# Keeping Newton iterates and row norms in PSUM in a hand-scheduled hybrid decoder layer, with the order planned again

## Chip, cores and metric

The kernel runs on one core of a Trainium2 chip. The time is device microseconds of one execution, median of several runs. Five engines run their own instruction queues side by side: PE (TensorE: matrix products into the accumulator memory PSUM), DVE (VectorE), ACT (ScalarE), POOL (GpSimd) and SP (SyncE, here the issuer of DMAs). [...]

## Reference

One decoder layer is applied to a prompt of 1024 tokens and to 8 sample tokens with caches. All data are float32. Cut to what the change touches:

```python
def rmsnorm(x, g):
    return x * lax.rsqrt(jnp.mean(x * x, axis=-1, keepdims=True) + NORM_EPS) * g

def decoder_layer(...):
    h = x + 0.5 * rmsnorm(swiglu(rmsnorm(x, n_ffn1_pre), ffn1_gate, ffn1_up, ffn1_down), n_ffn1_post)
    u = rmsnorm(h, n_mix_pre)
    proj = u @ w_in                    # q, k, v of group A, one row of 1792 for group B
    ...                                # partial rotary embedding
    ya = attend(q, k_all, v_all, ...)  # p = softmax(map 0) - lam * softmax(map 1), 4 heads
    ya = rmsnorm(ya, subln) * (1.0 - lam_init)
    yb, s_new, shift_new = rwkv7_time_mix(pb, prev, s0, lp)
    mix = concat([ya, yb]) @ w_out
    h = h + rmsnorm(mix, n_mix_post)
    h = h + 0.5 * rmsnorm(swiglu(rmsnorm(h, n_ffn2_pre), ffn2_gate, ffn2_up, ffn2_down), n_ffn2_post)

def rwkv7_time_mix(pb, prev, s0, lp):
    ...
    kk = kk / jnp.maximum(jnp.sqrt(jnp.sum(kk * kk, -1)), 1e-12)    # per head of 64
    s, y = wkv_scan(s0, r, decay, k, v, kk, a)                      # matrix state, 8 heads
    mean = jnp.mean(y, -1); var = jnp.mean(jnp.square(y - mean), -1)
    y = (y - mean) * lax.rsqrt(var + GN_EPS) * ln_x_w + ln_x_b      # per head
    ...
```

D_MODEL is 1024, the feed-forward width 2816, the two groups are 512 wide each, the past of a sample token 512.

## Kernel before

**Stages.** Tokens lie along the free axis in chunks of 256 or 264 columns, two chunks to a half of the prompt. There are four feed-forward phases: 0 and 1 are the first network for the two halves, 2 and 3 the second. `s_trunk` (L934) runs gate, up and down products of all phases (tiles `trunk_m`, `trunk_aux` in PSUM, sums of the outputs in `trunk_xl`, sums of squares in `trunk_acc`). A product is three matmuls of high and low parts, so each weight tile of 1024 columns is split on ACT (high part) and on DVE or POOL (low part: `wts_w`, `lin_w`). Behind each phase `s_tail` (L1165) takes one chunk at a time: norm of the output (`rstd`, L704: a matmul with `init_onesD`, a square root on ACT, a reciprocal on DVE), then `post` (L743: eight scalar_tensor_tensor on DVE and eight additions), then the next norm's input as high and low parts `tail_T` or `tail_xl`, which `s_project` (L1340, `proj_m`) multiplies. For group B, eight jobs of 128 tokens (`s_job`, L1556; `job`, L1565) make the delta-rule state; `init_ind` matmuls sum the squares of the keys, a Newton iteration on DVE (`rsqrt`, L712, on tiles of 128x8) turns them into a norm (`job_stf`), and near the end of a job the group norm needs the same again (`job_st`). `attend` (L2179) makes softmax rows, `s_finish` (L2233) the heads' norm (a Newton iteration on 128x4), `s_out`, `s_outnorm` (L1371, L1425) the output projection and its norm. The sample tokens' attention (`dec_cb`, `dec_dreg`; `a_decode`, L2260) and state step (`decb_dec`, `decb_dreg`; `b_decode`, L1901) run in between.

**Order.** These generators are streams. The kernel is built in dry passes; in each, a list scheduler (`run`, L456) takes the streams' instructions by due times (`latest`, L533), with a price for each (`price`, L362) and a table `BIAS` that shifts a stream's due time by so many microseconds. `price` knows that an operation of DVE with two wide SBUF inputs keeps POOL off and the other way round (`o.port`), and `either` (L406) puts a subtraction or addition on DVE or POOL by that account. PASSES is 3, and the plan with the smallest planned end is built. The result is one fixed order for every engine. All instructions are recorded at line 301 of before (305 of the changed file), so the views tell them apart by tiles.

A PSUM tile has one of eight banks of 512 columns; a stream owns names of banks (`m0`... , `aux0`, `aux1`, `cb`, `dec`), and a new tile in a bank waits for the last reader of the one before.

Of the kernel before, what the change touches and what calls it, by code (L numbers as in the profile page):

```python
# [22 lines left out]
P = 128  # L23
# [13 lines left out]
FOUR = 1  # L37
PARTS = 2
# [7 lines left out]
C = 64  # L46
# [45 lines left out]
PASSES = 3  # L92
BIAS = {"trunk2": 300, "outn3": -70, "outb0": 30, "pre2": 7, "prep1": 60, "resid0": -60, "outn1": -10, "pre3": 30, "outn0": 3, "pre1": 3, "job13": 60, "ldxb0": -60}
# [59 lines left out]
HOP = {"tensor": (0.0, 0.2, 0.2, 0.22, 0.2), "vector": (0.18, 0.127, 0.13, 0.155, 0.13), "scalar": (0.165, 0.14, 0.143, 0.165, 0.15),  # L153
# [42 lines left out]
class Kern:  # L196
# [159 lines left out]
    @staticmethod  # L356
    def after(d, o):

        return d.seen + HOP[d.eng][ENGINES.index(o.eng)] - (o.load if d.eng == "tensor" else 0.0) + MARG * (d.eng != o.eng)

    @staticmethod
    def price(o, op, a, k, out, ins):  # L362
# [30 lines left out]
        elif o.eng == "vector":  # L393
            wide = [x for x in ins if tuple(x.shape[1:]) != (1,) and x.space != PSUM]
            fast = op in ("tensor_copy", "tensor_scalar", "memset") and all(x.space != PSUM for x in (out, *ins)) and len(wide) < 2

            o.port = fast or len(wide) > 1
            o.cost = 0.07 + n / (160 if op == "reciprocal" else 480 if op == "tensor_tensor_scan" else 1920 if fast else 960) \
                + (0.05 if op == "scalar_tensor_tensor" else 0.06 * scalars)
        elif o.eng == "scalar":  # L400
            o.cost = (0.06 if ins[0].space == PSUM else 0.093) + n / 1195 + 0.093 * scalars + 0.093 * ("accum_out" in k)
        else:
            o.port = True
            o.cost = (0.2 if op == "scalar_tensor_tensor" else 0.156 if op == "tensor_tensor" else 0.06) + n / (470 if op == "tensor_tensor" else 960)

    def either(self, op, out, *a, engines=("vector", "gpsimd")):  # L406

        if self.cur is not None:
            best = None
            for e in engines:  # L410
                o = Op(e, None, None)
                self.price(o, op, (out,) + a, {}, out, [x for x in a if isinstance(x, bass.AP)])
                t = max(self.free[e], self.held["gpsimd" if e == "vector" else "vector"] if o.port else 0.0) + self.backlog[e] + o.cost
                if e == "gpsimd" and o.port:

                    t += o.cost
                if best is None or t < best[0]:
                    best = t, e
            engines = best[1:]
        eng = getattr(self.nc, engines[0])  # L420
        getattr(eng, "copy" if op == "tensor_copy" and engines[0] == "scalar" else op)(out, *a)
# [34 lines left out]
    def run(self):  # L456
# [5 lines left out]
        while self.streams:  # L462
# [52 lines left out]
            if o.dma:  # L515
                rings = max(rings, s + (1.69 if o.eng == "gpsimd" else 1.17)) + o.dma
                o.seen = rings + 2.0
# [40 lines left out]

    def split(self, raw, tag, a, parts=1):
# [3 lines left out]
        for i in range(0, n, n // parts):  # L563
            t = slice(i, i + n // parts)
            self.nc.scalar.copy(h[:, t], raw[:, t])
            self.either("tensor_tensor", l[:, t], raw[:, t], h[:, t].bitcast(F32), ALU.subtract)
# [137 lines left out]
    def rstd(self, acc, eps=0, scale=1.0):  # L704

        nc = self.nc
        ps = self.ps2()[:, :acc.shape[-1]]
        nc.tensor.matmul(ps, self.onesD, acc, start=True, stop=True)
        nc.scalar.activation(acc, ps, AF.Sqrt, bias=self.eps[:, eps:eps + 1], scale=scale)
        nc.vector.reciprocal(acc, acc)  # L710
# [223 lines left out]
    def s_trunk(self):  # L934
# [3 lines left out]
        for ph in range(4):  # L938
# [181 lines left out]
            if ph == 3:  # L1120
                self.cur.banks = few + ("aux1",)
# [43 lines left out]
    def s_tail(self, ph, c, acc, y):  # L1165
# [26 lines left out]
        self.post(acc, y, f"n_ffn{1 + ph // 2}_post", h0 + o, z, rs)  # L1192
# [372 lines left out]
    def job(self, pool, i, s, jb):  # L1565
# [613 lines left out]
    def attend(self, pool, rd, ii, b):  # L2179
# [10 lines left out]
        for j in range(2):  # L2190
# [12 lines left out]
            V.tensor_scalar(mx[:, j, 0:1], mx[:, j, 0:1], -0.125, None, ALU.mult)  # L2203
# [29 lines left out]
    def s_finish(self, pool, half):  # L2233
# [3 lines left out]
        for rd in range(4 * half, 4 * half + 4):  # L2237
# [275 lines left out]
```

## Time and profile before

| | |
|---|---|
| median of 3 runs | 2349.36 us (2342.42 to 2352.55) |
| the profiled execution, its own time | 2346.93 us |
| its span in the trace | 2345.1 us |
| mean granted TensorE clock | 0.983 |
| POOL busy | 1069.0 us (46%) |
| HBM read, written | 254.86 MB, 41.46 MB |

Outside the span lie 1.83 us of the profiled execution. "Busy" of an engine is its share of the span; tenths in the page's second part show in which fortieth of it the engine works. A row of the trace's timeline gives start, length, engine, line, operation, out<-in by tiles, shapes and count, and in brackets the idle time ahead with what ended it. The kernel has stages with different limits, so stretches of 10 and 100 us are read apart.

### The profile page before, as it was taken

To read this page: it belongs to the slowest core of one execution; us is meant where nothing else is said; L and a number is where in the kernel's file an instruction comes from. 1 tells how busy PE (TensorE), PEld (TensorE's weight loads), DVE (VectorE), ACT (ScalarE), POOL (GpSimd) and SP (SyncE) were. 2 spreads that over 40 slices of the span, in tenths; PEclk is the share of its full clock that TensorE was granted. 3 is DMA by queue.
4 is the path that set the end of the run, shared out by engine and by line. 5 is a ranking of instruction groups with operands and counts; after the bars stand their busy time and mean duration, and the time that the engine had idled before them with its cause. 6 is when DMAs were issued, how large, how long until landed. Compare 5 with 4: busy or idle time off the path is not lost.

```text
span 2345.1 us, 42680 instructions
## 1 busy us (share of the span) xinstructions
PE 2247.0 (96%) x15871; PEld 1996.0 (85%) x15871; DVE 1658.5 (71%) x3616; ACT 1078.9 (46%) x2182; POOL 1069.0 (46%) x868
## 2 busy tenths in 40 slices
PE   7999999999999999999899998999999999999998
PEld 6999999898887778898778866777777988999998
DVE  6587898846776776838874278765777577777786
ACT  5643444543444345434452235553566556444444
POOL 5454564543333665346641133433434365444444
PEclk9999999999999999999899999999999999999999
DMA  6423333444333674635544376323535534423332
GB/s 201 129 82 100 100 106 112 125 145 127 102 102 111 190 231 137 188 109 180 168 131 144 113 168 154 86 69 96 151 105 137 175 108 132 134 64 109 109 100 73
DMA packets 454520, 299.12 MB, mean 128 GB/s; under 512 B 81033, under 2 KB 414957, under 8 KB 454312
## 3 DMA queue, kind: packets, MB, share of 16 engines
q1 hardware_dynamic: 453704, 294.78, 43.9%
q8 instruction: 126, 2.06, 0.4%
q0 software_dynamic: 320, 1.08, 0.1%
q14 instruction: 82, 0.67, 0.1%
q10 hardware_dynamic: 288, 0.52, 0.1%
HBM read 254.86 MB, written 41.46 MB: 126 GB/s over the span
## 4 chain that ended last, share of the span: by engine, by line
PE 58%; DVE 8%; ACT 3%; DMA 2%; issue 2%; POOL 1%; SPq 1%; DVEq 0%; POOLq 0%; ACTq 0%
PE trunk_m L301 32%; PE proj_m L301 7%; PE trunk_aux L301 5%; PE job_aux L301 4%; PE out_m L301 2%; PE outb_m L301 2%; PE attn_m L301 2%; PE attn_aux L301 2%; DVE mix_T L301 1%; DVE job_st L301 1%; DMA dec_dreg<-in_cache_k_dram 1%; DVE trunk_xl L301 1%; PE job_dec L301 1%; SPq L301 1%; DVE dec_dreg L301 1%
## 5 line engine op out<-in xcount | busy, mean ns | idle before, releaser
L301 POOL TENSOR_TENSOR wts_w<-wts_raw,wts_w 128x1024 fp32r<-128x1024 f32 (+2 forms) x184 | 349.5, 1905 | 372.9 <-ACT wts_w L301 296.6
L301 PE MATMUL trunk_m<-trunk_xl,wts_w 128*128 128x256 f32 (+2 forms) x2670 | 454.5, 322 | 12.1 <-DVE trunk_xl L301 10.3
L301 PE MATMUL trunk_m<-pre_X,wts_w 128*128 128x512 f32 (+3 forms) x2400 | 447.7, 336 | 11.3 <-ACT pre_sq L301 3.3
L301 PEld LDWEIGHTS trunk_m<-trunk_xl,wts_w 128*128 128x128 f32 x2670 | 381.6, 190 | 50.2 <-DVE trunk_xl L301 12.9
L301 PEld LDWEIGHTS trunk_m<-pre_X,wts_w 128*128 128x128 f32 x2400 | 353.6, 191 | 53.5 <-issue 7.0
L301 PE MATMUL trunk_m<-pre_T,wts_w 128*128 128x512 f32 (+3 forms) x1920 | 372.7, 345 | 3.3 <-DVE trunk_xl L301 2.3
L301 ACT CAST wts_w<-wts_raw 128x1024 fp32r<-128x1024 f32 (+2 forms) x293 | 247.0, 855 | 272.1 <-PE trunk_m L301 187.1
L301 PEld LDWEIGHTS trunk_m<-pre_T,wts_w 128*128 128x128 f32 x1920 | 296.1, 190 | 42.0 <-issue 3.3
L301 DVE TENSOR_TENSOR trunk_xl<-trunk_xl,trunk_m 128x256 f32<-128x256 f32 (+2 forms) x346 | 164.2, 491 | 64.1 <-PE trunk_m L301 62.6
L301 PE MATMUL proj_m<-tail_xl,lin_w 128*128 128x256 f32 (+1 forms) x1248 | 167.7, 290 | 1.9 <-DVE init_E L301 1.5
L301 PEld LDWEIGHTS proj_m<-tail_xl,lin_w 128*128 128x128 f32 x1248 | 155.3, 190 | 10.9 <-issue 6.8
L301 PE MATMUL proj_m<-tail_T,lin_w 128*128 128x512 f32 (+1 forms) x672 | 151.6, 387 | 1.3 <-ACT tail_T L301 1.3
L301 PEld LDWEIGHTS proj_m<-tail_T,lin_w 128*128 128x128 f32 x672 | 122.9, 195 | 28.6 <-ACT tail_T L301 1.8
L301 POOL TENSOR_TENSOR trunk_xl<-trunk_t,trunk_xl 128x512 fp32r<-128x512 f32 (+3 forms) x79 | 86.4, 1095 | 126.7 <-ACT trunk_xl L301 126.3
L301 DVE TENSOR_TENSOR wts_w<-wts_raw,wts_w 128x1024 fp32r<-128x1024 f32 (+2 forms) x109 | 117.9, 1089 | 23.7 <-ACT wts_w L301 23.1
L301 POOL TENSOR_TENSOR wts_w<-wts_lraw,wts_w 128x512 fp32r<-128x512 f32 x48 | 64.9, 1354 | 50.8 <-ACT wts_w L301 50.5
L301 ACT CAST trunk_xl<-trunk_t 128x256 fp32r<-128x256 f32 (+2 forms) x103 | 49.8, 483 | 75.5 <-DVE trunk_t L301 75.3
L301 PE MATMUL trunk_aux<-trunk_xl,wts_w 128*128 128x256 f32 (+1 forms) x546 | 75.9, 284 | 0.4 <-DVE trunk_xl L301 0.4
L301 POOL TENSOR_TENSOR mix_T<-mix_T 128x512 f32<-128x512 f32 x32 | 37.8, 1183 | 76.7 <-DMA mix_T<-PT 71.4
L301 POOL TENSOR_TENSOR lin_w<-lin_raw,lin_w 128x1024 fp32r<-128x1024 f32 x18 | 43.5, 2418 | 61.6 <-ACT lin_w L301 52.1
L301 PEld LDWEIGHTS trunk_aux<-trunk_xl,wts_w 128*128 128x128 f32 x546 | 69.7, 189 | 0.6 <-DVE trunk_xl L301 0.6
L301 ACT CAST wts_w<-wts_lraw 128x512 fp32r<-128x512 f32 x88 | 51.9, 620 | 39.4 <-PE trunk_m L301 15.5
(626 smaller groups left out, 4390.2 us busy)
## 6 DMA issues: line engine op xcount, KB each, us to landing
wts_raw<-in_ffn_gate_dram SPq DMA_DIRECT2D x88, 512.0 KB
wts_raw<-in_ffn_up_dram SPq DMA_DIRECT2D x60, 512.0 KB
wts_raw<-in_ffn_down_dram SPq DMA_DIRECT2D x60, 384.0 KB
wts_raw<-in_ffn_down_dram SPq DMA_DIRECT2D x27, 512.0 KB
lin_raw<-in_w_in_dram SPq DMA_DIRECT2D x26, 512.0 KB
mix_T<-PT SPq DMA_DIRECT2D x37, 256.0 KB
wts_lraw<-in_ffn_down_dram SPq DMA_DIRECT2D x16, 512.0 KB
dec_dreg<-in_cache_k_dram SPq DMA_DIRECT2D x32, 256.0 KB
```

Of the source, the lines that this page charges most:

```text
L301: o = Op(eng, lambda: fn(*a, **k), st)
```

## The change

The Newton iteration of the jobs and of the heads' norm gets a version, `rsqrt_psum`, whose iterate lies in PSUM: of two tensor inputs one is in PSUM each time. It takes x and -x/2 as two tiles, so the callers make one more multiplication and the iteration has one less. The group norm's mean and sums lie in PSUM too. `rstd` takes a bank and leaves the reciprocal there; the tails and the output norms use it, and their `post` reads the norm from PSUM. In the tails the norm's matmul is now issued after the waits for setup, residual and jobs, not ahead of them. For phase 0, whose last down product used six banks, it now uses four. In `attend` the multiplication of the row maximum by -0.125 is on ACT instead of DVE (64 instructions of 128x1). The planner counts ports by each operation's tensor inputs, reckons one pass more and takes the last plan, and `BIAS` has other entries. `PIECE` (2048) is not below the width of any tile split, so `low` never cuts; `TV`, `LAND` and `MPE` have the values that stood there before.

```diff
-PASSES = 3
-BIAS = {"trunk2": 300, "outn3": -70, "outb0": 30, "pre2": 7, "prep1": 60, "resid0": -60, "outn1": -10, "pre3": 30, "outn0": 3, "pre1": 3, "job13": 60, "ldxb0": -60}
+PASSES = 4
+BIAS = {"trunk2": 300, "outn3": -60, "outb0": 30, "pre2": -3, "wts1": 3, "lin3": -10, "wts2": -60, "decb0": 60, "job12": -30}
...
-            wide = [x for x in ins if tuple(x.shape[1:]) != (1,) and x.space != PSUM]
+            two = (a[1], a[3]) if op == "scalar_tensor_tensor" else ins if op == "tensor_tensor" else [x for x in ins if tuple(x.shape[1:]) != (1,)]
+            wide = [x for x in two if x.space != PSUM]
...
-    def rstd(self, acc, eps=0, scale=1.0):
+    def rstd(self, acc, eps=0, scale=1.0, bank=None):
         nc = self.nc
-        ps = self.ps2()[:, :acc.shape[-1]]
+        ps = (self.ps(bank=bank) if bank else self.ps2())[:, :acc.shape[-1]]
         nc.tensor.matmul(ps, self.onesD, acc, start=True, stop=True)
         nc.scalar.activation(acc, ps, AF.Sqrt, bias=self.eps[:, eps:eps + 1], scale=scale)
-        nc.vector.reciprocal(acc, acc)
+        out = ps if bank else acc
+        nc.vector.reciprocal(out, acc)
+        return out
+
+    def rsqrt_psum(self, y, x, t, py):
+        V = self.nc.vector
+        yi = py.bitcast(I32)
+        V.tensor_scalar(yi, x[0].bitcast(I32), 1, None, ALU.logical_shift_right)
+        V.tensor_scalar(yi, yi, -1, 0x5f3759df, ALU.mult, ALU.add)
+        for i in range(3):
+            V.tensor_tensor(t, py, x[1], ALU.mult)
+            V.tensor_tensor(t, t, py, ALU.mult)
+            V.scalar_tensor_tensor(y if i == 2 else py, t, 1.5, py, ALU.add, ALU.mult)
...
-            if ph == 3:
-                self.cur.banks = few + ("aux1",)
+            if ph in FAST:
+                self.cur.banks = few + (("aux1",) if ph else ("m2", "m3"))
...
-        if ph == 0:
-            rb = self.rb[:, o:o + n]
-            for _ in range(2):
-                nc.vector.tensor_tensor(acc, acc, rb, ALU.mult)
-        self.rstd(acc, 2, 1.0 if ph else TINY ** -2)
-        if ph == 0:
-            nc.vector.tensor_tensor(acc, acc, rb, ALU.mult)
-        yield
         yield ("wait", "setup")
         yield ("wait", ("loaded", 1))
...
-        self.post(acc, y, f"n_ffn{1 + ph // 2}_post", h0 + o, z, rs)
+        if ph == 0:
+            rb = self.rb[:, o:o + n]
+            for _ in range(2):
+                nc.vector.tensor_tensor(acc, acc, rb, ALU.mult)
+        norm = self.rstd(acc, 2, 1.0 if ph else TINY ** -2, f"aux{c if ph < 2 else 0}")
+        if ph == 0:
+            nc.vector.tensor_tensor(norm, norm, rb, ALU.mult)
+        self.post(norm, y, f"n_ffn{1 + ph // 2}_post", h0 + o, z, rs)
...
     def s_outnorm(self, half, c, acc, y, st):
-        self.rstd(acc)
         if c:
             yield ("wait", ("stage", 2 + half, 0))
-        self.post(acc, y[c], "n_mix_post", FIRST[2 + half] + CHUNKS[2 + half][c][0])
+        self.post(self.rstd(acc, bank=f"aux{c}"), y[c], "n_mix_post", FIRST[2 + half] + CHUNKS[2 + half][c][0])
...
-        rn, sx, st = (x[:, j] for x in [self.T(pool, [P, 3, 8], "stf")] for j in range(3))
+        rn, sx, sh, st = (x[:, j] for x in [self.T(pool, [P, 4, 8], "stf")] for j in range(4))
         V.tensor_scalar(sx, ps[:, 0:8], 1e-30, None, ALU.max)
-        self.rsqrt(rn, sx, st)
+        V.tensor_scalar(sh, ps[:, 0:8], 1e-30, -0.5, ALU.max, ALU.mult)
+        self.rsqrt_psum(rn, (sx, sh), st, ps[:, 8:16])
...
+        pm, py = (x[:, 8 * j:8 * j + 8] for x in [self.ps2()] for j in range(2))
...
-        V.tensor_reduce(st[:, 1], y2, AX.X, ALU.add)
-        V.tensor_scalar(st[:, 1], st[:, 1], 1.0 / C, GN_EPS, ALU.mult, ALU.add)
-        self.rsqrt(st[:, 0], st[:, 1], st[:, 2])
-        V.tensor_tensor(YG, YG, st[:, 0].unsqueeze(2).broadcast_to([P, 8, C]), ALU.mult)
+        V.tensor_reduce(pm, y2, AX.X, ALU.add)
+        V.tensor_scalar(st[:, 0], pm, 1.0 / C, GN_EPS, ALU.mult, ALU.add)
+        V.tensor_scalar(st[:, 1], pm, -0.5 / C, -0.5 * GN_EPS, ALU.mult, ALU.add)
+        self.rsqrt_psum(py, (st[:, 0], st[:, 1]), st[:, 2], py)
+        V.tensor_tensor(YG, YG, py.unsqueeze(2).broadcast_to([P, 8, C]), ALU.mult)
...
-            V.tensor_scalar(mx[:, j, 0:1], mx[:, j, 0:1], -0.125, None, ALU.mult)
+            A.mul(mx[:, j, 0:1], mx[:, j, 0:1], -0.125)
...
-    nc = build(min(plans, key=lambda p: p[:2])[2], False)
+    nc = build(plans[-1][2], False)
```

The order changes on every engine; the number of matmuls stays 14561 as written. The low parts go from POOL to DVE in part: of the 1024-column ones in `wts_w` POOL has 70 instead of 75, DVE 61 instead of 56; of the 768-column ones POOL has 33 instead of 43, DVE 27 instead of 17. Loads of ACT's function tables go from 38 to 42.

**First place: PE at the end of phase 1.** Here the first chunk's norm is made (`tail_dec` or `tail_aux`, from `trunk_acc`), and the projection of the chunk (`proj_m` from `tail_T`) follows. Before, in the order of PE's queue:

```order
L301 MATMUL trunk_m_1515_12911<-trunk_xl_978_8303,wts_w_1480_12761 128x256 x9
L301 MATMUL trunk_m_1544_12956<-pre_X_1399_11820,wts_w_1510_12880 128x256
L301 MATMUL trunk_m_1544_12956<-pre_X_1400_11821,wts_w_1510_12880 128x256
L301 MATMUL tail_dec_12830<-trunk_acc_12611,init_onesD_76 128x256
L301 MATMUL dec_cb_12715<-init_onesD_76,dec_dreg_8886 128x1 x4
L301 MATMUL dec_cb_12896<-init_ident_69,dec_dreg_8886 32x128
L301 MATMUL proj_m_1538_12941<-tail_T_1495_12835,lin_w_1534_12937 128x256
L301 MATMUL dec_cb_13051<-dec_dreg_8886,init_onesD_76 128x32
L301 MATMUL proj_m_1538_12941<-tail_T_1496_12836,lin_w_1534_12937 128x256
```

And now, from the last nine products that end phase 1's down product:

```order
L305 MATMUL trunk_m_1525_12966<-trunk_xl_981_8319,wts_w_1493_12840 128x256 x5
L305 MATMUL tail_aux_1503_12906<-trunk_acc_12709,init_onesD_76 128x256
L305 MATMUL trunk_m_1525_12966<-trunk_xl_981_8319,wts_w_1493_12840 128x256 x4
L305 MATMUL trunk_m_1527_12984<-trunk_xl_981_8319,wts_w_1493_12840 128x256 x9
L305 MATMUL decb_dec_12597<-decb_dreg_12596,bset_wa_166 128x8
L305 MATMUL trunk_m_1556_13028<-pre_X_1389_11671,wts_w_1523_12957 128x256
L305 MATMUL trunk_m_1556_13028<-pre_X_1390_11672,wts_w_1523_12957 128x256
```

The sample tokens' attention (`dec_cb`) now stands wholly ahead of this place, and between the norm and the first `proj_m` there stand 55 matmuls (13 of the down product, one of `decb_dec`, 41 of the next phase's gate and up products) where there were the five of `dec_cb`. The second chunk's norm has 49 behind it (14, one and 34) before products of the projection come again.

**Second place: DVE between the last transposes and the decay products of a job.** PE's `job_dec` with `init_ident` gives the keys, DVE makes `mix_T` from them, and PE's `job_dec` with `init_bones` needs that; `job_st` is the group norm of the job before, `job_aux` and `job_hres` are a triangular solve of another. The job is the seventh of eight; its last rows ahead of that product, before:

```order
L301 TENSOR_SCALAR job_st_1760_15180<-job_st_1760_15180 128x8
L301 TENSOR_SCALAR mix_T_1556_13148<-mix_T_1556_13148,setup_cols_159,setup_omka_161 128x512
L301 TENSOR_TENSOR mix_T_1655_14291<-mix_T_1655_14291,job_st_1760_15180 128x512
L301 TENSOR_TENSOR mix_T_1555_13147<-mix_T_1555_13147,mix_T_1556_13148 128x512
L301 SCALAR_TENSOR_TENSOR mix_T_1556_13148<-mix_T_1556_13148,setup_cols_159,mix_T_1555_13147 128x512
L301 TENSOR_TENSOR wts_w_1744_15023<-wts_raw_14975,wts_w_1744_15023 128x1024
L301 TENSOR_REDUCE job_st_1760_15180<-mix_T_1655_14291 128x8
L301 SCALAR_TENSOR_TENSOR mix_T_1556_13148<-mix_T_1555_13147,setup_cols_159 128x512
```

And now:

```order
L305 TENSOR_SCALAR mix_T_1568_13253<-mix_T_1568_13253,setup_cols_159,setup_omka_161 128x512
L305 TENSOR_TENSOR job_aux_1730_14841<-job_aux_1730_14841,job_hres_14840 128x28
L305 TENSOR_TENSOR mix_T_1567_13252<-mix_T_1567_13252,mix_T_1568_13253 128x512
L305 TENSOR_TENSOR job_hres_14840<-job_lraw_14839,job_aux_1730_14841 128x2x27
L305 TENSOR_TENSOR job_aux_1730_14841<-job_aux_1730_14841,job_hres_14840 128x2x27
L305 TENSOR_TENSOR job_hres_14840<-job_lraw_14839,job_aux_1730_14841 128x2x26
L305 TENSOR_TENSOR mix_T_1671_14458<-mix_T_1671_14458,job_aux_1751_15068 128x512
L305 TENSOR_TENSOR job_aux_1730_14841<-job_aux_1730_14841,job_hres_14840 128x2x26
L305 SCALAR_TENSOR_TENSOR mix_T_1568_13253<-mix_T_1568_13253,setup_cols_159,mix_T_1567_13252 128x512
L305 TENSOR_TENSOR job_hres_14840<-job_lraw_14839,job_aux_1730_14841 128x2x25
L305 SCALAR_TENSOR_TENSOR mix_T_1568_13253<-mix_T_1567_13252,setup_cols_159 128x512
```

The group norm, the weight's low part, a `trunk_g` operation and one of `decb_dreg` have left this stretch. From the first operation on the transposed keys to the last row shown there stand now 7 operations of 512 columns and 13 narrow ones of the solve. On PE, between the transposes and the decay product, stand 17 `trunk_m` of 512 columns and 24 narrow `job_aux` products, where there were 37 and six.

More of the change, by code (lines that the diff above doesn't have):

```diff
@@ L37 @@
 FOUR = 1
+PIECE = 2048
 PARTS = 2
@@ L149 @@
 OTHER = {"vector": "gpsimd", "gpsimd": "vector"}
-HOP = {"tensor": (0.0, 0.2, 0.2, 0.22, 0.2), "vector": (0.18, 0.127, 0.13, 0.155, 0.13), "scalar": (0.165, 0.14, 0.143, 0.165, 0.15),
+TV = 0.2
+LAND = 2.0
+MPE = 0.0
+HOP = {"tensor": (0.0, TV, TV, 0.22, 0.2), "vector": (0.18, 0.127, 0.13, 0.155, 0.13), "scalar": (0.165, 0.14, 0.143, 0.165, 0.15),
        "gpsimd": (0.31, 0.08, 0.15, 0.12, 0.15), "sync": (0.2, 0.15, 0.15, 0.15, 0.0)}
@@ L357, in after @@
     def after(d, o):
-        return d.seen + HOP[d.eng][ENGINES.index(o.eng)] - (o.load if d.eng == "tensor" else 0.0) + MARG * (d.eng != o.eng)
+        return d.seen + HOP[d.eng][ENGINES.index(o.eng)] - (o.load if d.eng == "tensor" else 0.0) + MPE * (o.eng == "tensor" and d.eng != "tensor" and o.st.label != "trunk")
     @staticmethod
@@ L406, in either, with choose @@
     def either(self, op, out, *a, engines=("vector", "gpsimd")):
[L408 to L421, printed above, removed]
+        e = engines[0] if self.cur is None else self.choose(op, out, *a, engines=engines)
+        getattr(getattr(self.nc, e), "copy" if op == "tensor_copy" and e == "scalar" else op)(out, *a)
+    def choose(self, op, out, *a, engines=("vector", "gpsimd")):
+        best = None
+        for e in engines:
+            o = Op(e, None, None)
+            self.price(o, op, (out,) + a, {}, out, [x for x in a if isinstance(x, bass.AP)])
+            t = max(self.free[e], self.held["gpsimd" if e == "vector" else "vector"] if o.port else 0.0) + self.backlog[e] + o.cost
+            if e == "gpsimd" and o.port:
+                t += o.cost
+            if best is None or t < best[0]:
+                best = t, e
+        return best[1]
     def spawn(self, gen, label, prio, *banks, ahead=None):
@@ L516, in run @@
                 rings = max(rings, s + (1.69 if o.eng == "gpsimd" else 1.17)) + o.dma
-                o.seen = rings + 2.0
+                o.seen = rings + LAND
             o.st.q[o.eng].popleft()
@@ L557, in raw, with low @@
         return self.T(self.wp, [P, 1024], "raw", bufs=2)
+    def low(self, out, raw, h):
+        n = raw.shape[-1]
+        e = self.choose("tensor_tensor", out, raw, h)
+        step = PIECE if e == "gpsimd" else n
+        for i in range(0, n, step):
+            t = slice(i, min(i + step, n))
+            getattr(self.nc, e).tensor_tensor(out[:, t], raw[:, t], h[:, t], ALU.subtract)
     def split(self, raw, tag, a, parts=1):
@@ L565, in split @@
             self.nc.scalar.copy(h[:, t], raw[:, t])
-            self.either("tensor_tensor", l[:, t], raw[:, t], h[:, t].bitcast(F32), ALU.subtract)
+            self.low(l[:, t], raw[:, t], h[:, t].bitcast(F32))
         return [t.rearrange("p (a b) -> p a b", a=a) for t in (h, l)]
@@ L1809, in job @@
         st = J([P, 3, 8], "st")
-        V.tensor_reduce(st[:, 0], YG, AX.X, ALU.add)
-        V.tensor_scalar(st[:, 0], st[:, 0], 1.0 / C, None, ALU.mult)
-        V.tensor_tensor(YG, YG, st[:, 0].unsqueeze(2).broadcast_to([P, 8, C]), ALU.subtract)
+        pm, py = (x[:, 8 * j:8 * j + 8] for x in [self.ps2()] for j in range(2))
+        V.tensor_reduce(pm, YG, AX.X, ALU.add)
+        V.tensor_scalar(pm, pm, 1.0 / C, None, ALU.mult)
+        V.tensor_tensor(YG, YG, pm.unsqueeze(2).broadcast_to([P, 8, C]), ALU.subtract)
         yy = U.rearrange("p n h t -> p (n h t)")
@@ L2241, in s_finish @@
             ao, ssq = self.ao[rd % 2], self.ssq[rd]
-            V.tensor_scalar(ssq, ssq, 1.0 / P, EPS, ALU.mult, ALU.add)
             sx, st = (self.T(pool, [P, 4], f"sx{j}") for j in range(2))
-            self.rsqrt(sx, ssq, st)
+            px, py = (x[:, 4 * j:4 * j + 4] for x in [self.ps2()] for j in range(2))
+            V.tensor_scalar(px, ssq, 1.0 / P, EPS, ALU.mult, ALU.add)
+            V.tensor_scalar(ssq, px, -0.5, None, ALU.mult)
+            self.rsqrt_psum(sx, (px, ssq), st, py)
             self.either("tensor_tensor", ao, ao, sx.unsqueeze(2).broadcast_to([P, 4, P]), ALU.mult)
```

## Prediction

> **What bounds the kernel now.** I read the page first, then the span in stretches of 100 us, then the two bad stretches in steps of 10 us and as a timeline of PE, and last the waits of PE. The page's first part:
>
> ```profile
> PE 2247.0 (96%) x15871; PEld 1996.0 (85%) x15871; DVE 1658.5 (71%) x3616; ACT 1078.9 (46%) x2182; POOL 1069.0 (46%) x868
> ```
>
> PE sets the time: it is idle 2345.1 - 2247.0 = 98 us. The matmuls are the same before and after, so the change can only win what PE waits, or what it computes at a lower clock behind a wait. The stretches of 100 us (length, busy time of PE, PEld, DVE, ACT, POOL, granted clock, DMA share, GB/s) say where that is:
>
> ```profile
> 1000.00:1100.00 100.00, 100.00 (x578) 87.71 (x578) 58.20 (x92) 42.47 (x74) 57.24 (x51) 1.00 0.46 138
> 1100.00:1200.00 100.00, 84.42 (x553) 77.91 (x552) 84.60 (x163) 53.54 (x101) 64.04 (x61) 0.86 0.52 149
> ...
> 1400.00:1500.00 100.00, 91.03 (x677) 66.78 (x676) 78.10 (x198) 51.29 (x104) 40.44 (x30) 0.94 0.53 125
> ```
>
> A usual stretch has no hole. From 1100 on PE lacks 15.6 us, at a clock of 0.86; from 1400 on it lacks 9.0 us at 0.94. The first is the end of phase 1, where the norms, the next projection and the sample tokens' attention meet:
>
> ```profile
> 1140.00:1150.00 10.00, 6.74 (x43) 5.74 (x41) 8.51 (x20) 7.53 (x11) 4.76 (x5) 0.82 0.70 188
> 1150.00:1160.00 10.00, 2.36 (x8) 1.78 (x9) 9.90 (x20) 3.58 (x8) 5.76 (x6) 0.50 0.45 132
> 1160.00:1170.00 10.00, 10.00 (x72) 9.93 (x71) 9.10 (x14) 5.07 (x14) 8.15 (x9) 0.83 0.72 205
> 1170.00:1180.00 10.00, 6.23 (x37) 5.57 (x36) 8.38 (x16) 7.96 (x16) 3.60 (x5) 0.86 0.31 67
> 1180.00:1190.00 10.00, 9.37 (x47) 8.53 (x46) 9.96 (x17) 4.73 (x11) 7.96 (x9) 0.67 0.25 67
> 1190.00:1200.00 10.00, 10.00 (x74) 9.27 (x72) 6.57 (x12) 7.18 (x15) 8.48 (x7) 0.96 0.65 196
> ```
>
> ```profile
> 1139.73 3.83 PE L301 MATMUL trunk_m<-trunk_xl,wts_w 128*128 128x256 f32 x31
> ...
> 1145.98 0.84 PE L301 MATMUL tail_dec<-trunk_acc,init_onesD 128*128 128x256 f32 x2 [1.43 <-POOL trunk_acc L301]
> ...
> 1152.91 0.58 PE L301 MATMUL proj_m<-tail_T,lin_w 128*128 128x256 f32 x1 [1.12 <-ACT tail_T L301]
> 1158.61 0.64 PE L301 MATMUL dec_cb<-dec_dreg,init_onesD 128*128 128x32 f32 x2 [5.12 <-DVE dec_dreg L301]
> 1159.06 4.70 PE L301 MATMUL proj_m<-tail_T,lin_w 128*128 128x256 f32 x21
> ```
>
> At full clock a matmul of 256 columns takes 3.83 / 31 = 0.124 us; behind the hole it takes 4.70 / 21 = 0.224. Counted at 0.125 us each, the 281 matmuls of the six windows are 35 us of work in 60 us. By place: 1140 to 1160 holds 51 (6.4 us), so 13.6 us are lost; 1170 to 1190 holds 84 (10.5), so 9.5 are lost; the other two lose 1.8. **About 25 us are lost at this one place**, clock included. DVE is the engine that is waited for: it is 9.90 of 10 busy in the worst window.
>
> **The tail, step by step.** Before, nothing but `dec_cb` stands between the norm's matmul and the first `proj_m`, and the second `proj_m` stands behind a `dec_cb` that waits 5.12 us for DVE. The chain from the norm's matmul to the first `proj_m` lasts 1152.91 - 1145.98 = 6.9 us. The changed order puts 55 matmuls there, 55 x 0.125 = 6.9 us, and the attention of the sample tokens is done by then. So the first chunk's hole of 13.6 us can nearly close. What is late next is the rest of `tail_T`: eight tiles come one after another, each behind an operation of `post`, an addition and two splits, while few fillers stand between their products. I leave 5 us of the 13.6 lost: minus 8.6. The second chunk's norm gets 49 x 0.125 = 6.1 us of cover, in a stretch where DVE is 9.96 busy and now also makes more low parts (front: 61 and 27 of them, five and ten more). I leave 6 of the 9.5: minus 3.5. Together **-12 us**; bounds 0 (the holes move behind the fillers) and -23 (both close).
>
> The norm in PSUM does its part here, by making `post` shorter:
>
> ```profile
> L301 DVE SCALAR_TENSOR_TENSOR trunk_xl<-trunk_xl,setup_cols,trunk_acc x32: 467/617/2610, 1150.8 to 1997.5; 128x256 f32<-128x256 f32 x32
> L301 DVE TENSOR_TENSOR job_st<-job_st x48: 139/162/2374, 619.5 to 1651.9; 128x8 f32<-128x8 f32 x48
> ```
>
> (Nanoseconds: least, median, most.) Half of the 32 operations of `post` in the tails last over 0.617 us where 0.467 would do. Why, a moment in a job shows:
>
> ```profile
> 670.13 2.39 POOL L301 TENSOR_TENSOR lin_w<-lin_raw,lin_w 128x1024 fp32r<-128x1024 f32 x1 [8.98 <-ACT lin_w L301]
> ```
>
> ```profile
> 670.17 2.37 DVE L301 TENSOR_TENSOR job_st<-job_st 128x8 f32<-128x8 f32 x1
> ```
>
> Eight elements last 2.37 us because POOL's subtraction, begun 0.04 us earlier, keeps the second input away. With one input in PSUM that wait should go. It is inside the -12 above for the tails, and no further term.
>
> **The jobs.** The groups by form (busy us, mean ns) say what the wait costs in Newton steps:
>
> ```profile
> L301 DVE TENSOR_TENSOR job_st<-job_st 128x8 f32<-128x8 f32 x48 | 17.2, 359 | 0.4
> ```
>
> 48 x (359 - 162) = 9.5 us of DVE go from these; the other Newton operations have less. But PE waited for these chains only here (total us, times, longest):
>
> ```profile
> PE job_aux L301 <- DVE job_stf L301: 3.1, 1, 3.1
> ...
> PE job_aux L301 <- DVE job_st L301: 1.9, 1, 1.9
> ```
>
> Of these 5.0 us I take 3 as won, since the rest of each chain stays. What a PSUM operand costs instead: no Newton step of before has one. The nearest rows are two chains of dependent operations, the first in SBUF (five steps from its first start to its last), the second the solve, that reads and writes PSUM (four steps):
>
> ```profile
> 493.61 0.37 DVE L301 TENSOR_TENSOR job_stf<-job_stf 128x8 f32<-128x8 f32 x2
> ...
> 494.61 0.17 DVE L301 SCALAR_TENSOR_TENSOR job_stf<-job_stf 128x8 f32<-128x8 f32 x1
> ...
> 1448.76 0.18 DVE L301 TENSOR_TENSOR job_hres<-job_lraw,job_aux 128x30 f32<-128x30 f32 x1
> ...
> 1449.66 0.18 DVE L301 TENSOR_TENSOR job_hres<-job_lraw,job_aux 128x28 f32<-128x28 f32 x1
> ```
>
> That is 0.200 against 0.225 us a step. The 16 chains of 11 operations could so get 176 x 0.025 = 4.4 us dearer if all were waited for, and up to 9.5 cheaper. I take nothing: one step in twelve falls away, which pays for most of the 0.025.
>
> [...]
>
> The larger part is order. The seventh job waits three times:
>
> ```profile
> 1431.93 1.09 PE L301 MATMUL job_aux<-job_w,mix_T 64*64 64x128 f32 x16
> ...
> 1449.51 5.12 PE L301 MATMUL trunk_m<-pre_X,wts_w 128*128 128x512 f32 x21
> ...
> 1458.84 1.13 PE L301 MATMUL job_dec<-mix_T,init_bones 128*128 128x512 f32 x2 [2.82 <-DVE mix_T L301]
> 1461.35 2.07 PE L301 MATMUL job_dec<-bset_la,bset_wa 64*128 64x512 f32 x2 [1.39 <-DVE mix_T L301]
> 1465.90 1.08 PE L301 MATMUL job_aux<-init_ident,mix_T 128*128 128x128 f32 x4 [2.47 <-DVE job_hres L301]
> ```
>
> ```profile
> 1446.52 0.68 DVE L301 TENSOR_TENSOR mix_T<-mix_T,job_dec 128x512 f32<-128x512 f32 x1
> ...
> 1448.16 0.68 DVE L301 TENSOR_TENSOR mix_T<-mix_T 128x512 f32<-128x512 f32 x1
> ...
> 1458.04 0.74 DVE L301 SCALAR_TENSOR_TENSOR mix_T<-mix_T,setup_cols 128x512 f32<-128x512 f32 x1
> ```
>
> DVE needs 1458.78 - 1446.52 = 12.3 us from the transposed keys to the decay product's input. In the changed order 7 wide and 13 narrow operations stand there: a wide one starts 0.60 us ahead of the next (1448.16 to 1448.76), so 4.2 us, and 13 x 0.225 = 2.9, together 7.1. PE's cover is 17 x 5.12 / 21 + 3 x 1.09 = 7.4 us (24 products as written are 48 in the trace). So the 2.82 us go, and with the group norm and the sample tokens' steps out of the way some of the other 3.9: -4. Other jobs got shorter covers too, and I put +2 for them. Sum of the jobs **-5 us**, bounds -12 (these waits and half as much again) and +11 (below).
>
> **ACT and the rest.**
>
> ```profile
> L301 DVE TENSOR_SCALAR attn_mx<-attn_mx 128x1 f32<-128x1 f32 x64 | 9.2, 148 | 0.7
> L301 ACT ACT_TABLE_LOAD x38 | 48.8, 1283 | 9.7 <-DVE tail_T L301 3.0 <-DVE trunk_g L301 2.1 <-PE trunk_aux L301 1.7
> ```
>
> ```profile
> L301 ACT COPY job_ec<-mix_T x8: 201/203/210, 523.7 to 1561.5; 128x8 f32<-128x8 f32 x8
> ```
>
> ACT gains 64 x 0.203 = 13 us and four table loads, 4 x 1.283 = 5.1 us; DVE loses 9.2. Both chains go through one engine as before, and in these stretches PE has trunk matmuls to do; I put +1 (0 to +5, every table load in the path). The order of everything else is new, and a place that was tight by luck may open: +2, from -3 to +8, as the single waits of 1 to 3 us on a usual place of this trace. The bank of a norm is now held until the eighth `post`, 8 x 0.467 = 3.7 us; the matmuls behind it in the rows of the order use other banks, so I cost that at nothing.
>
> **Sum.** 2346.93 - 12 - 5 + 1 + 2 = 2332.9, against the profiled execution, which is 2.4 us below the median of the three runs: **2333 us**.
>
> **Rivals.**
> 1. The tail's holes only move. POOL's additions and the splits pace the eight `tail_T`, the fillers come first and the products wait after them. For it: in the window at 1150 DVE is full with more than `dec_dreg`. Against it: the wait of 5.12 us is gone by order. The tail then gives 3, the jobs 3 and the rest +2: 2343 us, no difference that can be measured.
> 2. The change does nothing that PE sees: POOL's hold is real, but 96% of PE hides it, and each replanned place gives as much as it takes: 2347 us.
> 3. Slower: the jobs' covers. The products between transposes and decay product are fewer in nearly every job. The trace's elapsed times there (first job 497.2 to 507.1, last 1504.7 to 1515.6) sum to 93 us over eight jobs; the work that the changed order puts there is 68 us by the trace's durations, 78 before. If DVE's chains there stay as long as they were, 93 - 68 = 25 are lost where 93 - 78 = 15 were: +10. With the table loads, +5, and nothing won in the tail: 2362 us. It decides from a DVE chain of 68 / 8 = 8.5 us per job.
>
> ```profile
> L301 PE MATMUL job_dec<-init_ident,mix_T x32: 270/272/329, 497.2 to 1504.7; 128*128 128x128 f32 x32
> L301 PE MATMUL job_dec<-mix_T,init_bones x16: 590/592/1192, 507.1 to 1515.6; 128*128 128x512 f32 x16
> ```
>
> **How the numbers follow.** Forecast 0.50, rival 1 0.27, rival 2 0.10, rival 3 0.13. A measurement of this kernel tells about 0.5%, 11.7 us, from no change. The forecast's own bounds are 2347 - 23 - 12 + 1 - 3 = 2310 and 2347; I cut the low end to 2314, as both full gains at once are unlikely, and reach up to 2356 through rivals 1 and 2 and the better half of rival 3. Faster 0.50 (most of the forecast, a little of rival 1), within 0.5% 0.39, slower 0.11.
>
> **What would show it.** Right: the windows at the first `proj_m` of phase 1 hold over 60 matmuls in 10 us at a clock near 1; no `job_st` operation of 8 columns lasts over 0.3 us; PE's wait for `dec_dreg` is gone; the decay product of the seventh job waits under 1 us. [...]

## The result and the profile after

| | median us | runs |
|---|---|---|
| before | 2347.09 | 2342.42 to 2352.55 (4) |
| changed | 2308.36 | 2305.37 to 2311.55 (4) |

The ratio is 0.9828, 95% interval 0.9808 to 0.9848: 38.7 us faster. Forecast were 14 us and a low end of 2314; the sign was right, the size less than half. The profiled execution took 2305.92 us.

The first part of the page, to be held against that of before: PE is idle 2304.2 - 2235.6 = 69 us in place of 98, and 11 us less busy (granted clock 0.992 in place of 0.983). DVE lost 57 us.

```profile
PE 2235.6 (97%) x15871; PEld 1986.6 (86%) x15871; DVE 1601.9 (70%) x3565; ACT 1094.1 (47%) x2248; POOL 1039.5 (45%) x857
```

The stretches of 100 us of the changed kernel, the two bad ones of before and the one ahead of the tail:

```profile
1000.00:1100.00 100.00, 96.06 (x429) 77.61 (x428) 84.30 (x170) 37.93 (x59) 56.65 (x45) 0.98 0.58 171
1100.00:1200.00 100.00, 93.37 (x603) 84.88 (x602) 68.71 (x136) 59.78 (x108) 54.18 (x55) 0.95 0.57 155
...
1400.00:1500.00 100.00, 94.92 (x793) 72.72 (x787) 69.25 (x226) 45.80 (x102) 32.94 (x24) 0.99 0.31 85
```

The end of phase 1 lacks 6.6 us in place of 15.6, but 1000 to 1100, which lacked nothing, now lacks 3.9. PE's timeline at the place that the prediction spoke of:

```profile
1136.22 0.60 PE L305 MATMUL tail_aux<-trunk_acc,init_onesD 128*128 128x256 f32 x2
1136.47 1.89 PE L305 MATMUL trunk_m<-trunk_xl,wts_w 128*128 128x256 f32 x13
1138.28 0.39 PE L305 MATMUL decb_dec<-decb_dreg,bset_wa 64*128 64x8 f32 x2
1138.82 5.09 PE L305 MATMUL trunk_m<-pre_X,wts_w 128*128 128x256 f32 x41
1143.74 0.32 PE L305 MATMUL proj_m<-tail_T,lin_w 128*128 128x256 f32 x1
1143.90 0.98 PE L305 MATMUL trunk_m<-pre_X,wts_w 128*128 128x256 f32 x7
1147.43 0.39 PE L305 MATMUL decb_dec<-decb_dreg,bset_g 128*128 128x8 f32 x2 [2.55 <-DVE decb_dreg L305]
...
1169.42 0.38 PE L305 MATMUL proj_m<-tail_T,lin_w 128*128 128x256 f32 x1 [1.99 <-ACT tail_T L305]
```

From the norm's matmul to the first `proj_m` 7.5 us pass without a hole; then comes one of 2.55 us, for the sample tokens' state step, and one of 1.99 at the second chunk. The windows of 10 us at this place hold 81 (from 1130), 56 (from 1140, with the first `proj_m`) and 55 matmuls, so the mark of 60 with a clock near 1 is met ahead of the `proj_m` and missed behind it. And ahead of the phase's end, where the sample tokens' attention went:

```profile
1090.32 0.38 PE L305 MATMUL dec_cb<-init_onesD,dec_dreg 128*128 128x1 f32 x2 [1.97 <-DVE dec_dreg L305]
```

The Newton iterations (least, median, most in ns): no operation of theirs lasts over 175 (172 in these rows), where single ones lasted over 2300.

```profile
L305 DVE TENSOR_TENSOR job_st<-job_aux,job_st x24: 151/166/168, 600.5 to 1605.0; 128x8 f32<-128x8 f32 x24
L305 DVE TENSOR_TENSOR job_st<-job_st,job_aux x24: 154/161/165, 600.7 to 1605.2; 128x8 f32<-128x8 f32 x24
L305 DVE SCALAR_TENSOR_TENSOR job_aux<-job_st,job_aux x24: 135/170/172, 600.9 to 1605.4; 128x8 f32<-128x8 f32 x24
```

**Where the 39 us are.** Give each matmul the usual distance to the next of its own kind (the median over both traces) and sum these up to a mark that both programs have; what the clock shows beyond that sum is lost, by idle time, a low clock (0.67 in the changed kernel's window from 1150) or changes of tile shape (from a product of 512 columns to one with a 64x64 tile 0.326 us pass in place of 0.233, median of 23 before). The two are single executions. Ahead of the first `proj_m` one kernel below (the jobs in PSUM, old order) has the same rows as before on PE, and its trace is 2.8 us shorter there, so a difference under 3 us says nothing. Whether a kind is taken by shape alone or by shape and tiles moves single differences by up to 1.6 us. By stage, in us:

| stage, from the mark before to | lost before | after | difference |
|---|---|---|---|
| first `proj_m` of half 0 | 34.6 | 32.5 | -2.1 |
| fourth job's decay product | 31.8 | 18.4 | -13.4 |
| first product of the output projection | 26.7 | 25.9 | -0.8 |
| norm at the end of phase 1 | 7.1 | 14.8 | +7.7 |
| fifth job's decay product (holds the tail) | 27.2 | 16.3 | -10.9 |
| eighth job's decay product | 36.4 | 29.8 | -6.6 |
| first product of the second output projection | 34.8 | 24.4 | -10.4 |
| norm at the end of phase 2 | 12.1 | 6.1 | -6.0 |
| end | 5.9 | 8.8 | +2.9 |

The stage with the tail gave what was forecast (-10.9, for -12), though 7.7 went back ahead of it. The jobs and the attention of half 1 behind them gave 30 us; 5 had been forecast for the jobs.

### The profile page after: what moved, and what is told of

Read it like the earlier page. It is cut to its first block, busy times and chain, and to the rows that moved or that the text cites. A ratio compares the mean times of both kernels' runs of the same rounds, so it can differ in the third digit from the quotient of the medians.

```text
span 2304.2 us, 42716 instructions
## 1 busy us (share of the span) xinstructions
PE 2235.6 (97%) x15871; PEld 1986.6 (86%) x15871; DVE 1601.9 (70%) x3565; ACT 1094.1 (47%) x2248; POOL 1039.5 (45%) x857
## 4 chain that ended last, share of the span: by engine, by line
PE 76%; DVE 9%; DMA 5%; ACT 4%; issue 3%; POOL 2%; SPq 1%; DVEq 0%; ACTq 0%; POOLq 0%
PE trunk_m L305 43%; PE proj_m L305 11%; PE trunk_aux L305 7%; PE job_aux L305 5%; PE out_m L305 2%; PE attn_m L305 2%; PE outb_m L305 2%; PE attn_aux L305 1%; DVE init_rb L305 1%; DVE trunk_xl L305 1%; ACT wts_w L305 1%; DMA mix_T<-PT 1%; DVE dec_dreg L305 1%; PE job_dec L305 1%; DVE mix_T L305 1%
## 5 line engine op out<-in xcount | busy, mean ns | idle before, releaser
L305 POOL TENSOR_TENSOR wts_w<-wts_raw,wts_w 128x1024 fp32r<-128x1024 f32 (+2 forms) x170 | 319.1, 1884 | 379.9 <-ACT wts_w L305 311.7
L305 PE MATMUL trunk_m<-trunk_xl,wts_w 128*128 128x256 f32 (+2 forms) x2700 | 459.7, 322 | 13.9 <-DVE trunk_xl L305 7.3
L305 DVE TENSOR_TENSOR wts_w<-wts_raw,wts_w 128x1024 fp32r<-128x1024 f32 (+2 forms) x123 | 133.3, 1088 | 41.5 <-ACT wts_w L305 40.2
L305 POOL TENSOR_TENSOR trunk_xl<-trunk_t,trunk_xl 128x512 fp32r<-128x512 f32 (+3 forms) x83 | 95.5, 1153 | 116.6 <-ACT trunk_xl L305 116.1
L305 DVE TENSOR_TENSOR trunk_t<-trunk_g,trunk_m 128x512 f32<-128x512 f32 (+2 forms) x77 | 42.9, 558 | 53.6 <-PE trunk_m L305 49.8
```

The lines of the kernel that those rows point to most:

```text
L305: o = Op(eng, lambda: fn(*a, **k), st)
```

## Experiments

A hold is the time by which an operation of DVE lasts longer because one of POOL runs beside it, as the 2.37 us of eight elements in the prediction, where the median is 0.162. POOL was held too: of its operations of 256 columns, 0.787 us by the median before, one lasted 1.46 beside a subtraction of 1024 columns on DVE (at 1005.40 us of that trace). Theory A: POOL's holds on the operations are the loss, and to remove them is the gain. Theory B: the gain is a better order, which the planner found. To part them, the order of a kernel was written out as a list, and other operations were built in that order: each queue keeps its rows one for one, so only durations and operands differ (where rows had to move, it is said). Times are medians; ratios are to runs of the kernel before on the same chip, with 95% intervals.

### Old operations in the new order

The iterations of jobs and heads back in SBUF, and with them the mean and the sums of the group norm:

```diff
-        self.rsqrt_psum(rn, (sx, sh), st, ps[:, 8:16])
+        self.rsqrt_psum(rn, (sx, sh), st, rn)
...
-        pm, py = (x[:, 8 * j:8 * j + 8] for x in [self.ps2()] for j in range(2))
+        self.ps2()
+        pm = py = st[:, 2]
...
-            px, py = (x[:, 4 * j:4 * j + 4] for x in [self.ps2()] for j in range(2))
+            self.ps2()
+            px, py = st, sx
```

> The changed kernel with every engine's order kept as it is, row for row, and only the Newton iterations of jobs and heads back in SBUF (the same number of instructions). If the gain is POOL's hold on these operations, the holds come back in the chains of all eight jobs: 10 to 20 us more than the changed kernel's 2308, and job_st operations of 8 columns that last 1 to 2.4 us. If the gain is the new order, 0 to 5 us more. [...]

2349.59 us, 1.0009 (0.9994 to 1.0024): 41 us over the changed kernel, twice the most that theory A had; the whole gain is gone. The holds are back, over 2 us in TENSOR_SCALAR too, which has one tensor input:

```profile
L487 DVE TENSOR_TENSOR job_st<-job_st x48: 154/166/2027, 602.0 to 1646.7; 128x8 f32<-128x8 f32 x48
L487 DVE TENSOR_SCALAR job_st<-job_st x40: 151/171/2216, 597.8 to 1643.0; 128x8 f32<-128x8 f32 x24, 128x8 int32<-128x8 int32 x16
```

One group norm shows how a hold reaches PE. Changed kernel, DVE, then PE:

```profile
770.77 0.69 DVE L305 TENSOR_REDUCE job_aux<-mix_X 128x8 f32<-128x512 f32 x1 [0.55 <-ACT mix_X L305]
...
778.76 0.69 DVE L305 TENSOR_TENSOR mix_X<-mix_X,job_aux 128x512 f32<-128x512 f32 x1
```

```profile
771.76 7.92 PE L305 MATMUL trunk_m<-pre_T,wts_w 128*128 128x512 f32 x33
779.59 0.63 PE L305 MATMUL job_aux<-init_ident,mix_X 128*128 128x128 f32 x4
```

The chain takes 8.7 us, and 33 matmuls cover it to the end. The same rows with the iteration in SBUF, DVE, POOL and PE:

```profile
788.47 0.69 DVE L487 TENSOR_REDUCE job_st<-mix_X 128x8 f32<-128x512 f32 x1 [0.54 <-ACT mix_X L487]
...
792.66 2.23 DVE L487 TENSOR_SCALAR job_st<-job_st 128x8 f32<-128x8 f32 x2
...
796.25 2.46 DVE L487 TENSOR_TENSOR job_st<-job_st 128x8 f32<-128x8 f32 x2
...
801.19 0.69 DVE L487 TENSOR_TENSOR mix_X<-mix_X,job_st 128x512 f32<-128x512 f32 x1
```

```profile
792.39 2.40 POOL L487 TENSOR_TENSOR wts_w<-wts_raw,wts_w 128x1024 fp32r<-128x1024 f32 x1 [2.50 <-ACT wts_w L487]
796.21 1.26 POOL L487 TENSOR_TENSOR trunk_xl<-trunk_t,trunk_xl 128x512 fp32r<-128x512 f32 x1 [1.42 <-ACT trunk_xl L487]
```

```profile
788.42 8.14 PE L487 MATMUL trunk_m<-pre_T,wts_w 128*128 128x512 f32 x33
802.03 1.09 PE L487 MATMUL job_aux<-init_ident,mix_X 128*128 128x128 f32 x4 [5.47 <-DVE mix_X L487]
```

The chain takes 13.4 us, the cover is the same 33 matmuls, and PE waits 5.47 us. The waits view books them on `mix_X`, the last link; `job_st`, which was held, does not appear.

The heads' iterations alone back in SBUF, which is the third pair of lines above:

> The changed kernel, row for row in its order, with only the heads' Newton iterations (four columns) back in SBUF; the jobs' stay in PSUM. If the 41 us of the first run are the jobs', 2308 to 2314. If the heads hold a good part of them, 2318 to 2335.

2311.98 us, 0.9838 (0.9816 to 0.9860): 2.3 us over the changed kernel by the ratios, less than the interval. So all but about 2 of the 41 us are the jobs'. The heads' operations are held all the same:

```profile
L487 DVE TENSOR_TENSOR fin_sx<-fin_sx,prep_ssq x24: 147/161/2378, 849.1 to 1779.8; 128x4 f32<-128x4 f32 x24
```

Over all 104 of them the holds add up to 9.3 us of DVE (what they last over 0.165 us), and PE hardly pays: not every hold is waited for.

The row norms back in SBUF:

```diff
-        out = ps if bank else acc
-        nc.vector.reciprocal(out, acc)
-        return out
+        nc.vector.reciprocal(acc, acc)
+        return acc
```

> The changed kernel in its own order with only the row norms of tails and output projections back in SBUF (reciprocal into the sums' tile; the next phase's first sum on POOL then follows the last post operation). If POOL's hold on post is what the tail lost, 5 to 10 us more than 2308, near the phase ends. If the order is what counts, 0 to 4 more.

2339.92 us, 0.9954 (0.9937 to 0.9972): 31.6 us over the changed kernel, three times the most that theory A had. An operation of `post` in the later tails has a median of 0.940 us in place of 0.474, here this run and then the changed kernel:

```profile
L487 DVE SCALAR_TENSOR_TENSOR trunk_xl<-trunk_xl,setup_cols,trunk_acc x32: 470/940/2578, 1156.1 to 1985.6; 128x256 f32<-128x256 f32 x32
```

```profile
L305 DVE SCALAR_TENSOR_TENSOR trunk_xl<-trunk_xl,setup_cols,tail_aux x16: 468/474/476, 1141.7 to 1169.1; 128x256 f32<-128x256 f32 x16
```

The 80 operations of `post` in tails and output norms last 30.7 us in all over 0.475 each, for 21.2 before and 0.3 in the changed kernel. The edit also lets the next phase's first sum of squares wait for the last `post`, since they share a tile again. That is not the loss: ACT's idle time ahead of the eight first sums is 9.5 us here and 9.4 in the changed kernel.

The loss table, made for this run (its profiled execution is 37 us longer), has the difference mostly where a norm stands: 3.8 us up to the first `proj_m`, 8.9 from the fourth job to phase 1's norm (the first output projection), 6.8 in the tail of phase 1, 16.0 from the second output projection on.

The multiplication of the row maxima back on DVE, and then all three groups:

```diff
-            A.mul(mx[:, j, 0:1], mx[:, j, 0:1], -0.125)
+            V.tensor_scalar(mx[:, j, 0:1], mx[:, j, 0:1], -0.125, None, ALU.mult)
```

> The changed kernel in its own order with the 64 multiplications of row maxima back on DVE. All theories: within 4 us of 2308; plus 1 to 3 if DVE is short in the attention stretch, minus 1 to 3 if ACT is.

2312.88 us, 0.9849 (0.9830 to 0.9868): intervals overlap with the changed kernel's; nothing that can be told.

> The changed kernel's order with all three groups of operations back in their old place (Newton and norms in SBUF, multiplication on DVE). Order theory: 2308 to 2318, so that the order holds 29 to 39 of the 38.7 us. Operation theory: 2330 to 2345, so that the order by itself is worth under 15 us.

2380.12 us, 1.0130 (1.0109 to 1.0152), above both expectations. The new order with the old operations is 1.3% slower than before: by itself it costs 31 us. And 41.2, 31.6 and 4.5 make 77, near the 72 between this run and the changed kernel, so the groups nearly add.

### New operations in the old order

All of them first (two banks differ at the end of phase 0, and a few rows wait for a bank):

> All operations of the changed kernel (Newton and norms in PSUM, multiplication on ACT), but every engine's order that of before, but for a few rows that wait for a bank. Theory that POOL's holds are the cost wherever they fall: most of the 38.7 us come without a new order, 2312 to 2325. Theory that the planner had already put POOL's work beside the holds, so that the gain needs both: 2332 to 2345.

2353.71 us, 1.0023 (1.0007 to 1.0039). No gain at all; both theories fall short. Then the iterations of jobs and heads alone, with the norms in SBUF and the multiplication on DVE:

> Only the Newton iterations in PSUM, in the order of before; norms in SBUF and multiplication on DVE as before. First theory: 20 to 30 us under before, from the jobs and the stretch behind them, as the opposite edit cost 41 in the new order. Second theory: 3 to 12 under before, of the size of the DVE time (18 us) that these operations lasted too long in before's profile.

2349.99 us, 1.0011 (0.9994 to 1.0028). Of PE's waits in the attention of half 1 a large one is new in both, here the first of these two runs (total us, times, longest):

```profile
PE fin_cb L488 <- POOL mix_T L488: 7.2, 3, 3.2
```

The heads' iteration takes a bank of its stream. Three of the eight iterations stand later in DVE's queue for it than in the last kernel of this part, which differs only in keeping them in SBUF; PE's queue is the same in both. The first one of half 1 starts at 1741.95 us of this trace in place of 1697.68, of which 9 us were lost by the eighth job already, and PE waits for the transposes (`fin_cb`) behind it. So, in the kernel before as it was, only the jobs:

```diff
-        self.rsqrt(rn, sx, st)
+        self.rsqrt_psum(rn, (sx, sh), st, ps[:, 8:16])
...
-        self.rsqrt(st[:, 0], st[:, 1], st[:, 2])
+        self.rsqrt_psum(py, (st[:, 0], st[:, 1]), st[:, 2], py)
```

> The kernel before, row for row in its old order, with only the eight jobs' Newton iterations and group norms' sums in PSUM (the heads' norm, which took a bank in the runs before this, is left as it was). The old order left DVE 21.5 us of holds on these operations. If a fixed order passes on what its waits of PE name, 3 to 6 us under before; if it passes on half of the holds, 9 to 13; if the bank that the group norm now takes costs PE, 0 or slower.

2334.28 us, 0.9943 (0.9927 to 0.9959): 13.4 us under before by the ratio, without a row of another operation moved, just over what half of the holds would give (9 to 13). And everything but the heads:

```diff
-            px, py = (x[:, 4 * j:4 * j + 4] for x in [self.ps2()] for j in range(2))
+            px, py = st, sx
```

> All operations of the changed kernel except the heads' in the order of before, but for a few rows that wait for a bank. If the heads' bank is what ate the gain in the old order, the jobs' 13 us are there and the norms add to them: 2322 to 2335. If norms and banks cost as much in the old order as they give, 2333 to 2345. If the fault lies elsewhere, 2345 to 2355.

2334.64 us, 0.9929 (0.9908 to 0.9951): 15 to 17 us under before, as expected if the heads' bank ate the gain. The value is also just inside the second expectation, and both hold in part: the norms add only 0 to 3 here, and to take the heads' bank cost 22 (1.0023 - 0.9929) in the old order.

### Planned anew

```diff
-PASSES = 3
-BIAS = {"trunk2": 300, "outn3": -70, "outb0": 30, "pre2": 7, "prep1": 60, "resid0": -60, "outn1": -10, "pre3": 30, "outn0": 3, "pre1": 3, "job13": 60, "ldxb0": -60}
+PASSES = 4
+BIAS = {"trunk2": 300, "outn3": -60, "outb0": 30, "pre2": -3, "wts1": 3, "lin3": -10, "wts2": -60, "decb0": 60, "job12": -30}
...
-    nc = build(min(plans, key=lambda p: p[:2])[2], False)
+    nc = build(plans[-1][2], False)
```

These lines alone, in the kernel before:

> The kernel before with only the planner's table, the number of passes and the choice of the last plan taken from the change, planned anew. If the table is worth something by itself: 2330 to 2340. If it is only good for the new operations: 2345 to 2365.

2392.55 us, 1.0195 (1.0163 to 1.0226). And the changed kernel with these lines taken back:

> The changed kernel with the planner's table, passes and choice of before, planned anew for the new operations. If the operations carry the gain, any plan that is made for them has most of it: 2305 to 2325. If the table carries it: 2330 to 2345.

2341.65 us, 0.9968 (0.9953 to 0.9983). With the old operations this table's plan is 45 us slower, more than expected, and the new operations planned by the old table give 0.3%. Is it the table, or chance? The changed kernel with PASSES = 3, and with 5:

> The changed kernel with three dry passes in place of four, and so the plan of the third: the same operations, the same table, another order. If the new operations and the table give the gain as such, 2305 to 2320. If the gain is that of one lucky order among many, 2328 to 2350.

2325.80 us, 0.9898 (0.9881 to 0.9915).

> The changed kernel with five dry passes, the plan of the fifth. As with three: 2305 to 2320 if any plan for these operations is as good, 2320 to 2345 if the fourth was a lucky one.

2321.91 us, 0.9889 (0.9873 to 0.9905). The first lies between its expectations, the second just inside that of a lucky fourth plan. Four plans for the same operations gave 0.32 (the old table), 1.02, 1.11 and 1.72%: one pass more or less moves the time by 14 to 17 us.

## Why the prediction was right and wrong

**The tail was right.** Step: 55 matmuls in place of five close the first hole. Measured: no wait ahead of the first `proj_m`, and -10.9 us for -12 in the stage that holds the tail. It is the order that did it: with the norms in PSUM but the old order (the last old-order kernel) this stage loses as much as before, within 0.2 us, and the norms in SBUF in the new order cost 6.8 there. What the step left out is that the sample tokens' attention only moved. The sign "PE's wait for `dec_dreg` is gone" did not come: 2.5 us of it stand ahead of the phase's end now, and that stage lost 7.7 more. Both together make -3.2, which is what rival 1 gave the tail, though by holes behind the fillers and not ahead of them.

**PSUM operands cost nothing here.** Step: "I take nothing", between +4.4 and -9.5. Measured: operations of 0.156 to 0.174 us for 0.160 to 0.171 (medians by form), and eight steps of the seventh job's iteration in 1.60 us, 0.200 each as in SBUF:

```profile
1406.96 0.17 DVE L305 TENSOR_TENSOR job_stf<-job_dec,job_stf 128x8 f32<-128x8 f32 x1
...
1408.56 0.16 DVE L305 SCALAR_TENSOR_TENSOR job_stf<-job_stf,job_dec 128x8 f32<-128x8 f32 x1
```

The upper bound of the jobs, +11, is a term that no run shows; in its place the runs showed these 0.200 us a step, and 13 us won by the jobs' iterations in the old order.

**The seventh job was right.** 7.1 us of DVE against 7.4 of cover were worked out; measured are 7.4 (1411.96 to 1419.37, the first and last of its operations) and no wait at the decay product, for 2.82 before:

```profile
1411.96 0.69 DVE L305 TENSOR_TENSOR mix_T<-mix_T,job_dec 128x512 f32<-128x512 f32 x1
...
1418.63 0.74 DVE L305 SCALAR_TENSOR_TENSOR mix_T<-mix_T,setup_cols 128x512 f32<-128x512 f32 x1
```

```profile
1419.43 1.12 PE L305 MATMUL job_dec<-mix_T,init_bones 128*128 128x512 f32 x2
```

**The step that failed first: "Of these 5.0 us I take 3 as won."** The holds went as the step said, and the term was too small: 13.4 us in the old order. It was too small for two reasons. First, the holds: I counted TENSOR_TENSOR alone (9.5 us) and called the rest less. Summed over all 216 small operations of both iterations in the trace of before, what they lasted over 0.165 us is 21.5 us (0.4 in the changed kernel), since TENSOR_SCALAR and SCALAR_TENSOR_TENSOR were held as well. I took it that POOL's operation keeps the second input away, but TENSOR_SCALAR has one and lasted up to 2.26 us in that trace, ending 0.025 us after a subtraction of POOL's. What the two engines share, no run here shows. Second, I took from the waits view only those waits that name the Newton tiles. A chain's wait is booked on its last link. Of 21.5 us of holds PE lost 13.4 in the old order; the waits that name them were 5.0.

**The step that failed as much: the order, above all that of the jobs ("-4", and "I put +2 for them").** The prediction has the order in three terms, -12 in the tail, -2 in the jobs and +2 for "everything else", -12 together. Two kernels above have the same operations, all new ones but the heads': 2334.64 us in the old order and 2311.98 in the new, 21 us by the ratios and 24 by their traces. A loss table of these two puts 11.7 of the 24 in the stage with the tail, as forecast, and 11.2 in the two stages of jobs, where 2 were forecast. The other six stages sum to -1.4, inside the range for "everything else", but by luck: they run from -10.0 (the attention of half 1) to +7.7. Four plans for the same operations spread over 33 us, so a range of 11 us for an order by this list scheduler was too narrow. All in all the term that failed is the sum of the jobs, -5 with bounds -12 and +11: their iterations gave 13 us and their order 11.

**Rival 3** said that thinner covers would cost if the chains kept their length. The time from the transposes to the decay products, 93.3 us over the eight jobs before, is 78.6 in the changed kernel. With the iterations back in SBUF it is 81.3, so only 2.7 of those 41 us lie at the place that rival 3 named. The same reasoning holds at the group norm shown above, where the chain grows by 4.7 us and PE waits 5.47.

**What was each worth?** One number for each does not exist. Medians in us (the multiplication of the row maxima, which gave nothing that can be told, is left out of account):

| in PSUM | old order | new order |
|---|---|---|
| nothing | 2347 | 2380 |
| jobs | 2334 | not run |
| jobs and norms | 2335 | 2312 |
| jobs and heads | 2350 | 2340 |
| norms | not run | 2350 |
| all | 2354 | 2308 |

The jobs' iterations are worth 13 us in the old order and, with the heads', 41 in the new one; the norms 0 to 3 and 32. The new order costs 31 us with the old operations, gives 21 with all but the heads' in PSUM and 46 with all, where the old order suffers from the heads' bank. The holds in the new order were not more by as much (28.0 us of excess on the jobs' operations with the iterations in SBUF, for 21.5 before). So each costs more there. That this is because the covers are cut to the new chains is shown at one place only, the group norm above.

**Open.** Whether the table was only the luckiest of many, or holds an entry that matters for a reason, was not told apart: no single entry was tried on the chip. The 7.7 us that went back ahead of the tail were not tried either; waits that name `dec_dreg` are 2.5 of them.

## What to carry to other kernels

When a kernel's order is planned to its operations' lengths, do not price a cheaper operation by the waits that carry its name. Sum what the operation lasts over its shortest, over all forms, and take this as what can be lost. How much of it PE pays depends on the order: here 13 of 21.5 us for the jobs and 0 to 3 of 21.2 for the norms in the old order, but in the new one some 39 of 28.0 for the jobs, 32 of 30.7 for the norms and about 2 of 9.3 for the heads. Treat a replanned order as a draw with a range of its own, some 15 us each way here, and try a few plans before an edit is judged. Building new operations in the old order's rows, and the old ones in the new rows, shows how far the two hang together; look first whether a new operation needs a bank that the old order does not have free, which hid the gain here.

## What was not expected of the hardware

The holds of the 8-column operations ended with POOL's operation beside them: 8 elements took up to 2.37 us beside a subtraction of 1024 columns that took 2.39. In the traces of before and of the first experiment, all 40 operations of 8 columns that lasted over 0.5 us ended 0.020 to 0.035 us after an operation of POOL. A wider one was held as well: one of `post`, 256 columns, took 2.61 us before, where 0.467 is the least, and ended 0.28 us after a subtraction of POOL's of 1024 columns. With one of two inputs in PSUM, in iterations that read and write PSUM in turn, none of the operations lasted over 0.175 us, with POOL 45% busy. And an iterate in PSUM was not slower than in SBUF: 0.200 us a step in both.
